# New instruction prices for the list scheduler of a one-layer hybrid encoder kernel

## The chip, the cores and the metric

The kernel runs on one core of one Trainium2 chip. The metric is the device time of one execution in microseconds; the figure given is the median over runs. A core has five engines that work from queues of their own, each in order: TensorE (matrix products), VectorE, ScalarE and GpSimd (elementwise work), and SyncE, which here issues the DMAs. In the profile they are PE (with PEld for the loading of weights), DVE, ACT, POOL and SP.

## The reference

One layer on 512 frames of width 1024, in float32. After an RMSNorm, one projection feeds three branches and their gates; the branches are merged, projected, added to the input, and a channel mixer follows:

```python
h = rmsnorm(x, norm_mix_g);  z = h @ w_in
# A: forgetting attention, 6 heads x 64, causal, bias from the summed log forget gates
logits = (q @ k.T) * scale + (c[:, None] - c[None, :]);  p = softmax(where(mask, logits, -inf))
# B: HGRN2, 4 heads, state 128 x 96, in chunks
attn = einsum(qx, kx, exp(b_t - b_s));  o = attn @ vx + (qx * exp(bx)) @ state
# C: gated input, causal depthwise convolution of width 31, LayerNorm, swish
merged = sigmoid(g0) * (ya @ wb0) + sigmoid(g1) * (yb @ wb1) + sigmoid(g2) * (yc @ wb2)
x = x + merged @ w_out
h2 = rmsnorm(x, norm_ffn_g);  gate, value = split(h2 @ w_up)
x = x + (silu(causal_dwconv3(gate)) * value) @ w_down
```

## The kernel before

Activations stand with channels on the 128 partitions and the 512 frames along the free dimension. Every large product is made in three float32r matmuls: weights and activations are split into a high and a low part, and high x high, high x low and low x high are summed in PSUM. A unit of weights (128 x 1024 float32) is loaded by a DMA (`wr_`), its high part is copied on ScalarE (`wh_`), and its low part is the difference on VectorE (`wl_`); one such unit feeds 24 matmuls of 512 columns, which fill one PSUM bank. VectorE then moves the bank to SBUF (`evac`) times the norm's factor.

The program has these stages. First the inputs are loaded and split, and the value product of the HGRN heads (`him`) runs with the norm's statistics. Then come the gated input of the convolution (`cb`, `ca`), the HGRN heads (`hf`, `hq`), the products of the attention (`f0`, `f1`, `fv`) and the output gate (`hg`). Beside these products the branches work on small tiles. An HGRN head (`hgrn_head`) takes exponentials and logarithms on ScalarE, a scan on VectorE (`b`), and then, for each of seven levels (the last without `d`), a difference on GpSimd (`d`), two exponentials on ScalarE (`ed`), two products on VectorE (`kl`, `ql`) and narrow float32 matmuls (`pl`). It also has a matmul on the products of first frames (`pr`, `pa`), transposes of `kh` (`khT`), and at the end `pi`. An attention head (`fox_head`) has differences on GpSimd (`dd`), `sp`, `ptp` and `po`. The convolution (`conv`) is 60 multiply-adds on VectorE (`cv`, the taps), started by two plain products. Then 24 gate products (`gl`), at most 18 of them ahead of the merges, the branch projections (`br`), the output projection (`wo`), the mixer (`ug`, `uv`) and the down projection (`dn`).

The order of all this is not written by hand. Class `Plan` records each instruction with its operands; `record` asks `cost` for two numbers, the time for which the instruction holds its engine and the time until others see its result. `schedule` then plays a list schedule: an instruction may start when its operands are there by these numbers, its engine is free, and the tiles that it is the first to write have a place under `CAPS`; among those that can start on an engine the lowest `pri` goes first. `pri` is the place in the program, less a large number for first loads (`FIRST`), weight preparation (`WPREP`), statistics and evacuation (`EVAC`). An instruction that can start is never held back for a more urgent one. `issue` emits the instructions in that order, and each engine and the DMA queue then run theirs in exactly that order, whatever the real durations are. All instructions are emitted from one line, so the profile shows nearly everything as L109 and is read by tile names.

Of the kernel before, what the change touches and what calls it, by code (L numbers as in the profile page):

```python
# [11 lines left out]
F32R = mybir.dt.float32r  # L12
# [51 lines left out]
class Plan:  # L64
    """Records the instructions, then issues them in the order of a list schedule.

    An instruction starts when its operands are there, its engine is free and the tiles that it
    is the first to write have a place; among those that can start, the lowest `pri` goes first.
    """

# [164 lines left out]
def cost(eng, name, outs, ins, args, kw):  # L235
    """Microseconds for which an instruction holds its engine, and until others see its result."""
    if name == "table":
        return 1.3, 0.1
    o = outs[0]
    n = 1  # L240
    for _, c in o.ap[1:]:
        n *= c
    hop = Plan.HOP
    if name == "dma_start":
        return max(0.45, o.ap[0][1] * n * 4 / 360e3), 2.1
    if eng == "tensor":
        wide = max(n, int(np.prod([c for _, c in ins[0].ap[1:]])))
        if name == "transpose":
            return 0.003 + wide * 0.835e-3, 0.3
        return 0.003 + wide * (0.4167e-3 if ins[0].dtype == F32R else 1.667e-3), 0.3  # L250
    psum = any(a.space == bass.MemoryType.PSUM for a in ins + outs)
    if eng == "scalar":
        aps = sum(isinstance(kw.get(k), bass.AP) for k in ("bias", "scale"))
        return (0.05 if psum else 0.1) + n * 0.833e-3 + 0.09 * aps + 0.087 * (kw.get("accum_out") is not None), hop
    if eng == "vector":
        aps = 0.058 * sum(all(c == 1 for _, c in a.ap[1:]) for a in ins) if n > 1 else 0.0
        if name in ("tensor_scalar", "tensor_copy", "memset", "tensor_single_scalar") and not psum:
            return 0.07 + n * 0.52e-3 + aps, hop
        if name == "reciprocal":
            return 0.07 + n * 6.2e-3, hop  # L260
        i = max([n] + [int(np.prod([c for _, c in a.ap[1:]])) for a in ins])
        return 0.07 + i * 1.04e-3 + aps, hop
    if name == "memset":
        return 0.06 + n * 0.8e-3, hop
    if name == "tensor_copy":
        return 0.1 + n * 3.5e-3, hop
    if any(s == 0 for a in ins for s, _ in a.ap[1:]):
        return 0.15 + n * 1.67e-3, hop
    return 0.15 + n * 2.1e-3, hop
# [3 lines left out]
def body(ctx: ExitStack, tc, xT, wct, wt3, wt1, wdn, par, cst, rst, msk, out):  # L273
# [9 lines left out]
    def nm(name):  # L283
        cnt[0] += 1
        return f"{name}_{cnt[0]}"
# [21 lines left out]
    def cc(name):  # L307
        o, w = CCOLS[name]
        return cs[:, o:o + w]

    ident, ones, big = cc("ident"), cc("ones"), cc("big")

# [1 line left out]
    def wunit(src, n, name, base=WPREP):  # L314
# [75 lines left out]
    def spread(cols, parts, name):  # L390
        """Columns [frame, (column of cols, block of frames)], each as a row that a run of partitions shares."""
        n = len(parts) * NM
        pt = bank(name + "rT")
        nc.tensor.transpose(pt[:n, :P], cols, ident)
        row = slot(name + "row")[:, :P]
        nc.vector.tensor_copy(row[:n], pt[:n, :P])
        dr = drp.tile([len(parts), NM, P], F32, name=nm(name + "dr"))
        nc.sync.dma_start(dr.rearrange("h m p -> (h m) p"), row[:n])
        t = slot(name + "rB")
        for u, (p0, p1) in enumerate(parts):  # L400
            nc.sync.dma_start(t[p0:p1], dr[u].rearrange("m p -> (m p)").unsqueeze(0).broadcast_to([p1 - p0, S]))
        return t
# [11 lines left out]

# [1 line left out]
    warm = slot("warm")  # L416
# [55 lines left out]

# [1 line left out]
    uus, first_sig = [], []  # L474
# [13 lines left out]

# [1 line left out]
    lbl = pc("lbl", 0, 4)  # L490
# [8 lines left out]
    lb = const("lbv", 4)  # L499
# [14 lines left out]

# [1 line left out]
    obs = []  # L516
# [6 lines left out]
    def hgrn_head(h, xf, xq):  # L523
# [4 lines left out]
        nc.vector.scalar_tensor_tensor(u, xf, 0.0, u, op0=ALU.min, op1=ALU.subtract)  # L528
        # forget gate: log f = logaddexp(log lb, log(1 - lb) + logsig)
        y = slot("y")  # L530
# [4 lines left out]
        nc.vector.tensor_tensor(lf, y, lf, op=ALU.add)  # L535
        # k = 1 - f
        kk = u
# [7 lines left out]
        nc.vector.tensor_tensor(qe, xq, eb, op=ALU.mult)  # L545
        # carried state
        kh = slot("kh")
# [16 lines left out]
        for c in range(1, NM - 1):  # L564
            nc.vector.scalar_tensor_tensor(st[:, c * HV:(c + 1) * HV], st[:, (c - 1) * HV:c * HV],
                                           eb[:, c * P + P - 1:c * P + P], pst[:, c * HV:(c + 1) * HV],
                                           op0=ALU.mult, op1=ALU.add)
        # attention inside a chunk, one level per power of two: in blocks of 2L frames the queries of
        # the second half see the keys of the first, and the first of those queries its own key
        at = ats[h % 2]  # L570
        atc = at.rearrange("p (c t) -> p c t", t=P)
        for li, L in enumerate(LEVELS):
# [20 lines left out]
            if L >= 32:  # L593
                # blocks that start at whole quadrants are taken one by one, and need no mask
                nb = P // (2 * L)
                for i in range(NM * nb):
                    nc.tensor.matmul(pl[:L + 1, i * L:(i + 1) * L], kl[:, 2 * i * L:2 * i * L + L + 1],
                                     ql[:, i * L:(i + 1) * L], start=True, stop=True)
                for i in range(nb):
                    o = 2 * i * L  # L600
                    nc.scalar.copy(atc[o:o + L + 1, :, o + L:o + 2 * L],
                                   pl[:L + 1, :S // 2].rearrange("p (c n l) -> p c n l", c=NM, l=L)[:, :, i])
                continue
            for c in range(NM):
# [6 lines left out]
                pl[:, :S // 2].rearrange("p (c n l) -> p c n l", c=NM, l=L))  # L611
        # the first frame of a chunk and its own key
        pr0 = tiny("pr0", NM)
# [41 lines left out]

# [1 line left out]
    tiles = ([], [])  # L657

    def fox_qk(qk):
# [23 lines left out]
        for j in range(3):  # L683
            pt = bank("qkT")
            for m in range(NM):
                nc.tensor.transpose(pt[:, m * P:(m + 1) * P], raw[m][:, j * P:(j + 1) * P], ident)
            # high parts of both heads, and for each head a tile with the high part in one half
            # of the partitions and the low part in the other
            one = slot(f"qk1{qk}{j}", F32R)
            two = [slot(f"qk2{qk}{j}", F32R) for _ in range(2)]  # L690
            if qk == 0:
                nc.scalar.activation(one, pt, AF.Copy, scale=g)
            for r, t in zip((0, FD), two):
                rs, ro = slice(r, r + FD), slice(FD - r, P - r)
                if qk == 0:
                    hi, lo = one[rs], t[rs]
                else:
                    hi, lo = t[rs], one[rs]
                    nc.scalar.activation(hi, pt[rs], AF.Copy, scale=g[rs])
                nc.vector.scalar_tensor_tensor(lo, pt[rs], g[rs], hi.bitcast(F32), op0=ALU.mult, op1=ALU.subtract)  # L700
                nc.vector.tensor_copy(t[ro], one[rs])
            tiles[qk].append((one, two))
# [5 lines left out]
    def fox_v():  # L708
        pss = gemm_t([wt1[u] for u in range(4)], FW + FH, "fv")
        lfx = tiny("lfx", NM * FH)  # L710
        for m, ps in enumerate(pss):
            with nc.at(EVAC):
                # even heads, then odd ones: high and low parts side by side, for the odd heads low parts first
                two = [slot(f"fv{m}{a}", F32R) for a in range(2)]
# [32 lines left out]
    def fox_head(h):  # L747
# [8 lines left out]
        last = []  # L756
        # the transposed weights of two blocks of queries lie side by side for each block of keys
        for i0 in (0, 2):
            ptps = [bank(f"ptp{h}{i0}{a}") for a in range(i0 // 2 + 1)]
            for i in (i0, i0 + 1):  # L760
# [12 lines left out]
                                               accum_out=mn)  # L773
# [15 lines left out]
            for k in range(i0 + 2):  # L789
                n = 2 * P if k <= i0 else P  # L790
                w = fv[k][h % 2][:, j * P:(j + 1) * P]
                for u in range(2):
                    with nc.after(*last):
                        op = nc.tensor.matmul(po[:, (i0 + 2) * P - n:(i0 + 2) * P], w,
                                              pts[k // 2][u][:, k % 2 * 2 * P:k % 2 * 2 * P + n],
                                              start=k == u == 0, stop=k == i0 + 1 and u == 1)
# [7 lines left out]

# [1 line left out]
    zs = []  # L806
# [45 lines left out]

# [1 line left out]
    hgrn_head(0, *hgrn_gemm(0))  # L854
# [32 lines left out]

# [1 line left out]
    bounds = ((0, 3), (3, 6), (6, 8))  # L889
# [33 lines left out]

# [1 line left out]
    acc2 = None  # L925
# [13 lines left out]

# [1 line left out]
    gT = []  # L941
# [14 lines left out]
    for n in range(KT):  # L956
        parts = ((0, S),) if n < KT - 1 else ((0, S // 2), (S // 2, S))
# [91 lines left out]
```

## Time and profile before

| | us |
|---|---|
| median of three runs | 843.89 |
| lowest, highest run | 841.92, 846.9 |
| profiled execution, first to last instruction | 844.6 |
| TensorE busy (PE) | 821.4 |
| VectorE busy (DVE) | 512.6 |
| ScalarE busy (ACT) | 333.2 |
| GpSimd busy (POOL) | 161.5 |

The profile is of one execution, and gives no other time of it than this span. Busy time is the time in which an engine had an instruction in work; a busy TensorE is not one at its peak. The granted clock (PEclk) is the share of TensorE's full clock that it was given in a stretch.

### The profile page before, as it was taken

To read this page: it belongs to the slowest core of one execution; us is meant where nothing else is said; L and a number is where in the kernel's file an instruction comes from. 1 tells how busy PE (TensorE), PEld (TensorE's weight loads), DVE (VectorE), ACT (ScalarE), POOL (GpSimd) and SP (SyncE) were. 2 spreads that over 40 slices of the span, in tenths; PEclk is the share of its full clock that TensorE was granted. 3 is DMA by queue.
4 is the path that set the end of the run, shared out by engine and by line. 5 is a ranking of instruction groups with operands and counts; after the bars stand their busy time and mean duration, and the time that the engine had idled before them with its cause. 6 is when DMAs were issued, how large, how long until landed. Compare 5 with 4: busy or idle time off the path is not lost.

```text
span 844.6 us, 10337 instructions
## 1 busy us (share of the span) xinstructions
PE 821.4 (97%) x3979; PEld 690.2 (82%) x3979; DVE 512.6 (61%) x813; ACT 333.2 (39%) x536; POOL 161.5 (19%) x144
## 2 busy tenths in 40 slices
PE   6998989999999999999999999999999999999998
PEld 5887989867777788888888888888888888888888
DVE  6589998998877873355664456555555555322221
ACT  6235464645555653333233334333333333212110
POOL 4215040055542200011352311111100111000000
PEclk9998999989999999999999999999999999999999
DMA  6622122321111232223443223233332223333320
GB/s 214 193 75 70 49 66 76 104 90 46 63 64 58 68 100 94 92 103 112 137 137 100 99 88 100 100 100 101 100 100 89 92 94 94 109 103 119 119 82 26
DMA packets 26238, 80.74 MB, mean 96 GB/s; under 512 B 2982, under 2 KB 3782, under 8 KB 26188
## 3 DMA queue, kind: packets, MB, share of 16 engines
q1 hardware_dynamic: 26188, 80.08, 29.2%
q8 instruction: 31, 0.51, 0.3%
q14 instruction: 19, 0.16, 0.1%
HBM read 77.94 MB, written 2.13 MB: 95 GB/s over the span
## 4 chain that ended last, share of the span: by engine, by line
PE 87%; DVE 9%; issue 2%; ACT 1%; DMA 1%; POOL 0%; SPq 0%; DVEq 0%
PE gl L109 15%; PE dn L109 14%; PE ug L109 14%; PE uv L109 14%; PE wo L109 5%; PE br L109 5%; PE pl L109 2%; PE fvm L109 2%; PE hg L109 2%; PE sp L109 2%; DVE qk L109 1%; PE cb L109 1%; PE ca L109 1%; PE hf L109 1%; DVE cv L109 1%
## 5 line engine op out<-in xcount | busy, mean ns | idle before, releaser
L109 POOL TENSOR_TENSOR fy<-fy,n2rB 128x512 f32<-128x512 f32 x22 | 29.2, 1328 | 207.4 <-ACT fy L109 207.4
L109 DVE TENSOR_TENSOR wl_wd<-wr_wd,wh_wd 128x1024 fp32r<-128x1024 f32 (+1 forms) x24 | 27.3, 1136 | 65.8 <-ACT wh_wd L109 65.8
L109 DVE TENSOR_TENSOR wl_ug<-wr_ug,wh_ug 128x1024 fp32r<-128x1024 f32 x22 | 27.2, 1237 | 53.5 <-ACT wh_ug L109 53.5
L109 ACT CAST wh_wd<-wr_wd 128x1024 fp32r<-128x1024 f32 (+1 forms) x24 | 23.5, 980 | 85.7 <-PE dn L109 81.9
L109 ACT CAST wh_gl<-wr_gl 128x1024 fp32r<-128x1024 f32 x24 | 25.2, 1050 | 59.8 <-issue 49.7
L109 POOL TENSOR_TENSOR gr<-gr,gr 128x512 f32<-128x512 f32 x16 | 25.1, 1567 | 123.5 <-DVE gr L109 122.7
L109 DVE TENSOR_TENSOR gr<-gl,n1rB 128x512 f32<-128x512 f32 x24 | 16.6, 691 | 50.4 <-PE gl L109 50.2
L109 DVE SCALAR_TENSOR_TENSOR cv<-xca,pr,cv 128x511 f32<-128x511 f32 (+29 forms) x60 | 46.5, 780 | 0.2
L109 ACT CAST wh_uv<-wr_uv 128x1024 fp32r<-128x1024 f32 x22 | 23.2, 1053 | 45.6 <-PE ug L109 38.2
L109 POOL TENSOR_TENSOR d<-b 128x512 f32<-128x512 f32 x24 | 34.3, 1453 | 17.8 <-DVE b L109 9.3
L109 ACT CAST wh_ug<-wr_ug 128x1024 fp32r<-128x1024 f32 x22 | 23.1, 1050 | 27.6 <-PE uv L109 21.2
L109 DVE TENSOR_TENSOR wl_gl<-wr_gl,wh_gl 128x1024 fp32r<-128x1024 f32 x24 | 31.5, 1311 | 3.2 <-ACT wh_gl L109 2.7
L109 POOL TENSOR_TENSOR dd<-cB,cq 128x128 f32<-128x128 f32 (+3 forms) x24 | 18.7, 783 | 76.1 <-DMA cB<-cdr 50.4
L109 DVE SCALAR_TENSOR_TENSOR fy<-ug,pr,fy 128x511 f32<-128x511 f32 (+1 forms) x44 | 32.6, 747 | 0.7
L109 DVE TENSOR_TENSOR ug<-ug,n2rB 128x512 f32<-128x512 f32 x22 | 15.2, 692 | 28.9 <-PE ug L109 27.3
L109 ACT ACTIVATE fy<-fy 128x512 f32<-128x512 f32 x22 | 13.9, 632 | 41.3 <-DVE fy L109 41.3
L109 DVE TENSOR_TENSOR wl_uv<-wr_uv,wh_uv 128x1024 fp32r<-128x1024 f32 x22 | 27.0, 1225 | 4.2 <-ACT wh_uv L109 4.2
L109 PEld LDWEIGHTS pl<-ql,kl 128*128 128x128 f32 (+2 forms) x224 | 21.9, 171 | 5.6 <-POOL d L109 3.9
L109 PE MATMUL pl<-ql,kl 128*128 128x64 f32 (+2 forms) x224 | 22.6, 254 | 3.3 <-DVE ql L109 3.2
L109 DVE TENSOR_TENSOR x<-dn,x 128x512 f32<-128x512 f32 (+1 forms) x9 | 5.7, 632 | 27.8 <-PE dn L109 27.8
L109 DVE TENSOR_TENSOR gr<-gr,br 128x512 f32<-128x512 f32 x24 | 16.2, 683 | 6.7 <-PE br L109 6.7
L109 DVE TENSOR_TENSOR kl<-ed,u 128x260 f32<-128x260 f32 (+6 forms) x28 | 17.4, 621 | 3.3 <-issue 3.0
(1128 smaller groups left out, 2654.4 us busy)
## 6 DMA issues: line engine op xcount, KB each, us to landing
wr_gl<-wct SPq DMA_DIRECT2D x24, 512.0 KB, 3.3
wr_ug<-wct SPq DMA_DIRECT2D x22, 512.0 KB, 3.3
wr_uv<-wct SPq DMA_DIRECT2D x22, 512.0 KB, 3.2
wr_wd<-wdn SPq DMA_DIRECT2D x16, 512.0 KB, 3.5
x<-xT SPq DMA_DIRECT2D x16, 256.0 KB, 3.6
wr_wb<-wct SPq DMA_DIRECT2D x8, 512.0 KB, 3.4
wr_wo<-wct SPq DMA_DIRECT2D x8, 512.0 KB, 3.3
wr_wd<-wdn SPq DMA_DIRECT2D x8, 384.0 KB, 3.1
```

What stands on the lines that cost most here:

```text
L109: op.fn = lambda: fn(*args, **kw)
```

## The change

It changes the numbers that `cost` gives for VectorE, ScalarE and the wide matmuls, and gives the scan a price of its own. The other lines of the diff take out comments. Prices of GpSimd and of the DMAs, the delay until others see a result, the priorities and the caps stay.

```diff
...
-        return 0.003 + wide * (0.4167e-3 if ins[0].dtype == F32R else 1.667e-3), 0.3
+        if ins[0].dtype == F32R:
+            return 0.013 + wide * 0.4167e-3, 0.3
+        return 0.003 + wide * 1.667e-3, 0.3
     psum = any(a.space == bass.MemoryType.PSUM for a in ins + outs)
     if eng == "scalar":
         aps = sum(isinstance(kw.get(k), bass.AP) for k in ("bias", "scale"))
-        return (0.05 if psum else 0.1) + n * 0.833e-3 + 0.09 * aps + 0.087 * (kw.get("accum_out") is not None), hop
+        return (0.143 if psum else 0.187) + n * 0.833e-3 + 0.09 * aps + 0.087 * (kw.get("accum_out") is not None), hop
     if eng == "vector":
         aps = 0.058 * sum(all(c == 1 for _, c in a.ap[1:]) for a in ins) if n > 1 else 0.0
         if name in ("tensor_scalar", "tensor_copy", "memset", "tensor_single_scalar") and not psum:
-            return 0.07 + n * 0.52e-3 + aps, hop
+            return 0.155 + n * 0.52e-3 + aps, hop
         if name == "reciprocal":
-            return 0.07 + n * 6.2e-3, hop
+            return 0.145 + n * 6.2e-3, hop
+        if name == "tensor_tensor_scan":
+            return 0.145 + n * 2.08e-3, hop
         i = max([n] + [int(np.prod([c for _, c in a.ap[1:]])) for a in ins])
-        return 0.07 + i * 1.04e-3 + aps, hop
+        return 0.155 + i * 1.04e-3 + aps, hop
...
```

## Rows read from the trace of the kernel before

**Rows 1.** The head of the page.

```profile
span 844.6 us, 10337 instructions
```

**Rows 2.** Windows by stage: stretch, length, busy (count) PE, PEld, DVE, ACT, POOL; PEclk, DMA, GB/s.

```profile
0.00:20.00 20.00, 13.96 (x62) 11.75 (x62) 13.01 (x15) 14.59 (x23) 7.88 (x10) 1.00 0.68 226
20.00:306.00 286.00, 272.04 (x1491) 233.00 (x1492) 247.92 (x499) 146.15 (x305) 86.73 (x90) 0.95 0.25 79
306.00:840.00 534.00, 534.00 (x2417) 444.26 (x2417) 251.20 (x300) 172.44 (x210) 66.86 (x45) 1.00 0.31 100
840.00:844.60 4.60, 1.43 (x12) 1.22 (x11) 0.42 (x1) 0.00 (x0) 0.00 (x0) 0.99 0.08 29
```

**Rows 3.** Windows of 20 us between 20 and 306 us, the same columns.

```profile
20.00:40.00 20.00, 19.32 (x92) 17.56 (x93) 11.40 (x19) 5.21 (x8) 7.17 (x9) 0.91 0.59 188
...
60.00:80.00 20.00, 16.14 (x93) 14.38 (x92) 19.74 (x25) 11.26 (x22) 10.96 (x7) 0.91 0.23 73
80.00:100.00 20.00, 20.00 (x129) 19.00 (x128) 18.98 (x39) 9.91 (x23) 0.00 (x0) 0.92 0.21 61
...
120.00:140.00 20.00, 17.78 (x123) 16.71 (x123) 17.54 (x37) 11.13 (x26) 3.18 (x3) 0.91 0.23 73
...
160.00:180.00 20.00, 18.34 (x90) 14.71 (x87) 19.61 (x29) 12.23 (x18) 6.23 (x7) 1.00 0.29 95
180.00:200.00 20.00, 19.57 (x90) 14.52 (x91) 16.66 (x31) 10.86 (x26) 11.49 (x9) 0.74 0.20 64
200.00:220.00 20.00, 17.15 (x98) 13.54 (x97) 20.00 (x36) 10.30 (x32) 15.14 (x17) 1.00 0.16 55
220.00:240.00 20.00, 19.91 (x148) 18.02 (x148) 15.43 (x38) 9.79 (x26) 7.39 (x12) 0.92 0.13 42
...
280.00:300.00 20.00, 18.25 (x89) 14.81 (x88) 18.64 (x43) 14.49 (x24) 4.70 (x3) 1.00 0.29 93
```

**Rows 4.** Waits of TensorE over the span: us in total, times, longest.

```profile
PE pl L109 <- DVE ql L109: 3.2, 2, 2.3
...
PE pa L109 <- DVE pr L109: 2.8, 2, 2.1
...
PE khT L109 <- DVE kh L109: 2.2, 1, 2.2
```

**Rows 5.** Timeline of TensorE in 174 to 190 us: start, us, instruction [idle before].

```profile
180.43 0.19 PE L109 MATMUL pa<-pr,cs 128*1 128x4 f32 x2 [2.09 <-DVE pr L109]
180.55 0.50 PE L109 MATMUL hq<-x6l,wh_hq 128*128 128x512 f32 x1
```

**Rows 6.** Groups by form: out<-in, shapes, count | busy us, mean ns | idle before.

```profile
L109 DVE TENSOR_TENSOR wl_uv<-wr_uv,wh_uv 128x1024 fp32r<-128x1024 f32 x22 | 27.0, 1225 | 4.2 <-ACT wh_uv L109 4.2
...
L109 DVE TENSOR_TENSOR gr<-gl,n1rB 128x512 f32<-128x512 f32 x24 | 16.6, 691 | 50.4 <-PE gl L109 50.2
...
L109 DVE TENSOR_TENSOR ql<-ed,xq 128x256 f32<-128x256 f32 x24 | 13.8, 574 | 0.0
...
L109 DVE TENSOR_TENSOR_SCAN b<-reset,lf 128x512 f32<-128x512 f32 x4 | 4.9, 1213 | 0.0
...
L109 ACT CAST wh_gl<-wr_gl 128x1024 fp32r<-128x1024 f32 x24 | 25.2, 1050 | 59.8 <-issue 49.7 <-PE gl L109 6.4 <-PE hg L109 3.7
...
L109 POOL TENSOR_TENSOR d<-b 128x512 f32<-128x512 f32 x24 | 34.3, 1453 | 17.8 <-DVE b L109 9.3 <-PE sp L109 4.3 <-DVE rl L109 2.7
```

**Rows 7.** The chain that ended last: start, us, what.

```profile
305.98 54.41 PE gl L109 x240
360.40 5.44 PE br L109 x24
```

**Rows 8.** Timelines of VectorE and GpSimd in 46 to 82 us.

```profile
74.20 0.94 DVE L109 TENSOR_TENSOR kl<-ed,u 128x260 f32<-128x260 f32 x1 [0.26 <-ACT ed L109]
75.06 1.29 DVE L109 TENSOR_TENSOR ql<-ed,xq 128x256 f32<-128x256 f32 x1
...
70.01 9.66 POOL L109 TENSOR_TENSOR d<-b 128x512 f32<-128x512 f32 x6 [4.00 <-DVE b L109]
```

## The prediction

> **What bounds the kernel now.** I read the span first [rows 1]: 844.6 us for the profiled execution. The page gives no other time of that execution, so the sum is made against this span. The three timed runs have a median of 843.89, 0.7 less than the span and well inside their own 5 us of spread, so I carry a difference from the one to the other unchanged.
>
> Then the windows by stage [rows 2]. The reader is to see that the span has two parts that behave differently. From 306 to 840 us TensorE is busy for 534.00 of 534.00 us at a granted clock of 1.00, while VectorE is busy for 251.20 and ScalarE for 172.44. Nothing there waits, so no order of VectorE or ScalarE work can shorten it; only something that makes TensorE wait can lengthen it. From 20 to 306 us TensorE is busy for 272.04 of 286.00 us, and VectorE for 247.92. So 13.96 us of TensorE idle time lie here, and the clock averages 0.95. The first 20 us have 6.04 us more of idle time, with the DMA share at 0.68: that is loading.
>
> Next the same part in stretches of 20 us [rows 3]. Two prices stand in each row: idle time (20 less PE busy) and lost clock (20 times one less PEclk). Paired by place, a clock loss going with the stall before it:
> - head, 20 to 40: 0.68 + 1.8 = 2.5
> - A, 60 to 100: 3.86 + 1.8 + 1.6 = 7.3
> - B, 120 to 140: 2.22 + 1.8 = 4.0
> - C, 160 to 200: 1.66 + 0.43 + 5.2 = 7.3
> - D, 200 to 240: 2.85 + 0.09 + 1.6 = 4.5
> - E, 280 to 300: 1.75 and no clock loss
>
> The sum is 27.4 (some 0.4 of idle time lies in stretches not shown). A granted clock below 1.00 in these averages is time at the lower of two levels, 1.2 instead of 2.4 GHz, and in these rows it shows in a stretch in which TensorE had stood or in the next one. So a stalled microsecond costs about two: 13.96 idle and 13.8 lost clock.
>
> Last, what the stalls wait for [rows 4]: small results of VectorE, the ql, pr and kh of the HGRN heads. The timeline of C shows how it happens [rows 5]: two tiny matmuls on pr hold TensorE for 2.09 us, and behind them stands hq, whose operands are there. TensorE takes its queue in order; the planner had put pa ahead of hq because, by its prices, pr was ready by then.
>
> **The change part by part.** No operation, priority, tile or dependence changes. Only the prices by which the list schedule orders the queues do. I check each against a row [rows 6].
>
> VectorE's fixed part rises by 0.085 (0.075 for reciprocal and scan). A 128x512 product: old 0.07 + 512 x 1.04e-3 = 0.602, new 0.687, row 691 ns. A 128x1024 low part: new 1.220, row 1225. The scan: old 0.602, new 0.145 + 512 x 2.08e-3 = 1.210, row 1213. ScalarE: a 128x1024 cast was 0.953, now 1.040, row 1050. The wide matmul: old 0.003 + 512 x 0.4167e-3 = 0.2163, new 0.2263; 24 of them take 5.44 us [rows 7], 0.2267 each. So the new prices are those of instructions that run undisturbed.
>
> What the old prices hid in the middle part: 499 VectorE instructions x 0.085 = 42.4 us, on an engine that really works 247.92 of 286 us, against at most 1491 x 0.010 = 14.9 us of TensorE. VectorE fell behind TensorE by the difference, less its own idle time (38.1 us), and wherever it was behind, a branch matmul put "just in time" became a stall. The planner also filled gaps of VectorE that did not exist with taps of the convolution (60 of them, non-preemptive), ahead of work that TensorE was to wait for. With true prices those taps go later, the branch matmuls move back in TensorE's queue, and GEMM work fills in front of them. The filler is there: after 306 us ten units of gl run alone for 54.41 us before the first br [rows 7]; any of them can be taken earlier at no cost.
>
> What the change leaves wrong: GpSimd's prices, and any instruction that is stretched by a neighbour. A d of 128x512 has a broadcast operand and is priced 0.15 + 512 x 1.67e-3 = 1.005; its row says 1453 ns, 0.448 more, 24 times: 10.8 us. A ql of 128x256 is now priced 0.421 and takes 574 on the mean, 0.153 more, 24 times: 3.7 us. The timeline of A shows the bad case [rows 8]: while GpSimd runs six d in a row for 9.66 us, a kl of 260 columns takes 0.94 us (price 0.425) and a ql 1.29 (price 0.421), two and three times their prices.
>
> The Trainium skill (GPSIMD Engine Reference, 1. Specifications) says that GpSimd shares its SBUF interfaces with VectorE and that they contend when the VectorE instruction reads two SBUF inputs. The trace agrees with that as far as [rows 8] go. By that rule, no fixed price per instruction can place the kl and ql of a head rightly, and the stalls at the bursts would stay; its time is worked out as the second rival.
>
> So by stretch. B, C and E go: GpSimd is busy there for 3.18, 6.23 and 11.49, and 4.70 of 20 us, mostly less than in A and D (10.96 and 15.14), and the lag is mainly the one that the new prices know: -(4.0 + 7.3 + 1.75) = -13.05. Bounds: 0 if every one moves elsewhere, -13.05 if all go. A and D: the unpriced part remains. I take half of 7.3 + 4.5, so -5.9; bounds 0 and -11.8, half because these stretches hold both causes. Head: loading sets it; 0, bounds -2.5 and +2.5. New stalls that the new order makes: the trace cannot show them. Bounds 0 and 29.0 (10.8 + 3.7 unpriced, doubled for the clock); I take 6, near the price of one stall like A or C, since the order must change in hundreds of places and the four bursts stay. From 306 us on: 0, hidden under 534 us of matmuls; if the cover failed, one late low part would cost up to its own 1.225 us per unit. Prices of ScalarE: 0 by themselves, because ScalarE is busy for only 146.15 of 286 us; without that cover the cost would be a just-in-time stall as above, in the same terms.
>
> Sum: -13.05 - 5.9 + 6 = -13, so 831 us.
>
> **Rivals.**
>
> First, everything goes: all of A to E (24.9), no new stall: 844.6 - 24.9 = 820. For it: the filler of 54.41 us, and that no wait of TensorE but those on small VectorE results is long in this part. Against it: the 14.5 us unpriced.
>
> Second, the stalls only move. The unpriced 10.8 + 3.7 = 14.5 us reach TensorE whole, doubled by the clock: 29.0 against the 27.4 of today, so 846, no change. For it: [rows 8] is where A lies, and a list schedule leaves a branch matmul no slack. Against it: VectorE has 38.1 us of idle time in which lag can be absorbed, and GpSimd is busy for only 86.73 of these 286 us [rows 2].
>
> Third, slower: the taps of the convolution move out of the HGRN heads, VectorE then does kl and ql close together, right under the bursts of d, and every one of the four heads pays what A pays now: 4 x 7.3 = 29.2. With the head (2.5) and one long clock loss like the 5.2 of C this is 36.9 against 27.4, so 854 us. It decides from 24.9 / 4 = 6.2 us per head on; below that the kernel is not slower. For it: A is the costliest stall of today together with C, and is of this kind. Against it: D is also under a burst, the longest one, and costs 4.5. A second way to slower is weaker: VectorE priced full, the branches end so late that gl is used up. The branches would have to end 54.41 us later, more than the 42.4 that all new VectorE prices add; it has 0.02 within the chance below.
>
> **How the numbers follow.** A measurement of this kernel can tell about 0.5% from no change, here 4.2 us, so faster means below 839.7 and slower above 848.1. The forecast (gain of 5 to 20 us) has 0.48, the first rival 0.14, both faster: 0.62. The second rival has 0.20, the third 0.18. The range: the first rival's 820 lies near the low end; 818 leaves about 0.05 below, for a shorter head. Above, half of the third rival's 0.18 lies over 850. So 818 to 850, with the forecast's own range 825 to 839.
>
> **What would show it.** Right: in the part before the long run of gl, idle time of TensorE falls from 13.96 to about 8, the clock of that part rises above 0.95, and fewer stretches show it below 1.00; the waits on pr and kh vanish, those on ql shrink but stay; the taps of the convolution lie later; the run of pure gl before the first br is shorter than 54.41 us because some of it was used as filler; from there to the end nothing changes. Wrong in step: stalls of the B and C kind persist although VectorE's prices now fit (then VectorE's fixed part was not their cause), or kl and ql are stretched in all four heads (third rival), or TensorE is seen idle after the branches. The whole is wrong if the idle time and the clock loss fall and the span does not: then TensorE's busy time has grown by as much, through more changes between narrow and wide matmuls, which I price at nothing.

## The result, and the profile after

The kernel with the new prices takes 831.18 us (median of 4 runs, 830.0 to 832.68) against 845.33 (841.92 to 846.9) beside it: a ratio of 0.9844 with a 95% interval of 0.9809 to 0.9879. It is faster by 1.6%, and the forecast was 831. The profiled execution has a span of 830.0 us, so 14.6 of it are to be explained.

The windows of 20 us of the kernel after, with the columns of [rows 3]: stretch, length, busy time and count of PE, PEld, DVE, ACT, POOL, then PEclk, DMA share, GB/s.

```profile
0.00:20.00 20.00, 15.54 (x75) 14.10 (x76) 11.76 (x17) 13.85 (x21) 4.51 (x7) 1.00 0.72 240
20.00:40.00 20.00, 17.68 (x90) 15.20 (x89) 10.60 (x17) 6.49 (x11) 12.46 (x12) 1.00 0.53 177
...
60.00:80.00 20.00, 16.75 (x97) 15.58 (x95) 19.97 (x24) 9.91 (x18) 10.75 (x7) 0.99 0.25 85
80.00:100.00 20.00, 20.00 (x134) 18.32 (x134) 16.79 (x37) 11.05 (x27) 0.00 (x0) 0.93 0.19 57
...
120.00:140.00 20.00, 20.00 (x149) 19.62 (x148) 17.82 (x36) 11.19 (x28) 2.59 (x3) 1.00 0.30 106
...
160.00:180.00 20.00, 19.37 (x80) 14.59 (x79) 19.55 (x27) 9.75 (x14) 6.91 (x7) 0.91 0.24 82
180.00:200.00 20.00, 18.73 (x110) 14.68 (x109) 17.40 (x28) 11.84 (x28) 13.56 (x11) 1.00 0.20 67
200.00:220.00 20.00, 18.26 (x127) 15.18 (x127) 20.00 (x39) 11.47 (x33) 10.29 (x10) 1.00 0.16 53
220.00:240.00 20.00, 20.00 (x127) 16.66 (x126) 19.48 (x41) 10.12 (x29) 12.60 (x19) 1.00 0.17 54
...
280.00:300.00 20.00, 19.66 (x103) 15.74 (x102) 17.44 (x34) 14.00 (x27) 5.15 (x3) 1.00 0.20 70
```

The stretch of 120 to 140 us has no stall left (17.78 us busy before, [rows 3]), and PEclk is below 1.00 only in or right behind the stalls at 60 to 80 and at 160 to 180 us. VectorE is as busy as before, 512.4 us in all against 512.6: its work is the same, only its order differs. Over the first 460 us TensorE is idle for 14.0 us (20.0 before), and the mean granted clock of the span is 0.996 (0.984), so lost clock is 830.0 x 0.004 = 3.3 us against 13.5. The clock gave back more (10.2 us) than the idle time did (6.0 us).

What TensorE waited for in the kernel after (us in total, times, longest):

```profile
PE him L109 <- ACT wh_hi L109: 3.3, 2, 2.3
PE pl L109 <- DVE ql L109: 2.5, 3, 1.4
PE n1ms L109 <- POOL n1sq L109: 2.3, 1, 2.3
PE khT L109 <- DVE kh L109: 1.9, 1, 1.9
...
PE pa L109 <- DVE mn L109: 0.6, 1, 0.6
```

The wait on pr [rows 4] is gone, and those on ql are shorter. The wait on kh of [rows 4] lay at 120 to 140 us and is gone too, but another kh now makes TensorE wait for 1.9 us at 60 to 80 us. In the head the wait for the norm's statistics on GpSimd is new, in place of one on wl_hi.

The chain of the kernel after, around the first br:

```profile
296.25 16.18 PE gl L109 x71
312.43 0.44 PE cvt L109 x4
312.87 13.86 PE gl L109 x61
...
328.54 17.24 PE gl L109 x76
345.78 5.44 PE br L109 x24
```

The first br starts at 345.78 us instead of 360.40 [rows 7]: 14.6 us earlier, which is the whole gain. From there to the end both kernels take 484.2 us. The gates are now broken up by work of the convolution (cvt, ycT), because its taps run later. The tile cv in the kernel before, then in the kernel after (duration ns least/median/most, first and last start):

```profile
L109 DVE SCALAR_TENSOR_TENSOR cv<-xca,pr,cv x60: 697/733/1517, 45.7 to 215.5; 128x511 f32<-128x511 f32 x2, 128x510 f32<-128x510 f32 x2, 128x509 f32<-128x509 f32 x2, 128x508 f32<-128x508 f32 x2
```

```profile
L109 DVE SCALAR_TENSOR_TENSOR cv<-xca,pr,cv x60: 706/732/1779, 47.6 to 310.2; 128x511 f32<-128x511 f32 x2, 128x510 f32<-128x510 f32 x2, 128x509 f32<-128x509 f32 x2, 128x508 f32<-128x508 f32 x2
```

The last tap starts at 310.2 instead of 215.5 us.

### The profile page after: what moved, and what is told of

It is laid out like the page before. It is cut to its first block, busy times and chain, and to the rows that moved or that the text cites. A ratio compares the mean times of both kernels' runs of the same rounds, so it can differ in the third digit from the quotient of the medians.

```text
span 830.0 us, 10340 instructions
## 1 busy us (share of the span) xinstructions
PE 812.9 (98%) x3979; PEld 683.0 (82%) x3979; DVE 512.4 (62%) x813; ACT 332.7 (40%) x536; POOL 168.4 (20%) x144
## 4 chain that ended last, share of the span: by engine, by line
PE 89%; DVE 6%; issue 2%; POOL 1%; DMA 1%; ACT 1%; SPq 0%; DVEq 0%; POOLq 0%
PE gl L109 15%; PE dn L109 15%; PE ug L109 14%; PE uv L109 14%; PE wo L109 5%; PE br L109 5%; PE fvm L109 2%; PE pl L109 2%; PE f1m L109 2%; PE hf L109 2%; PE hq L109 2%; PE sp L109 2%; PE f0m L109 1%; PE ca L109 1%; PE cb L109 1%
## 5 line engine op out<-in xcount | busy, mean ns | idle before, releaser
L109 DVE SCALAR_TENSOR_TENSOR cv<-xca,pr,cv 128x511 f32<-128x511 f32 (+29 forms) x60 | 49.0, 827 | 0.2
L109 POOL TENSOR_TENSOR dd<-cB,cq 128x128 f32<-128x128 f32 (+3 forms) x24 | 22.0, 923 | 66.9 <-DVE u L109 38.2
L109 ACT ACTIVATE ed<-d 128x256 f32<-128x256 f32 x48 | 18.5, 413 | 5.5 <-POOL d L109 2.0
```

The costliest lines, as they stand in the source:

```text
L109: op.fn = lambda: fn(*args, **kw)
```

## The experiments

Theory L: instructions of VectorE took longer than planned, so results came later than their place in TensorE's queue, and each such lateness became a stall and a loss of clock. Rivals: the matmul price (P), ScalarE's price (S), the nearness of each price to the trace as such (A), an unlucky order before, against which any new one gains (C), and others named where they apply. Each kernel was timed in five rounds against the kernel before.

**One part alone.** The kernel before with one of the three groups of new prices.

```diff
-            return 0.07 + n * 0.52e-3 + aps, hop
+            return 0.155 + n * 0.52e-3 + aps, hop
...
-        return 0.07 + i * 1.04e-3 + aps, hop
+        return 0.155 + i * 1.04e-3 + aps, hop
```

> Only VectorE's prices are the new ones. Theory L (VectorE's lag against its plan is what became stalls): nearly the whole gain is here; ratio 0.978 to 0.988 to the kernel before, idle time of TensorE up to the first br about 14 us against 20.0, at most two stretches at 1.2 GHz. Rival P (the matmul price paces the plan): ratio 0.995 to 1.005. Rival S (ScalarE): the same, 0.995 to 1.005. Rival C (any new order would do, the order before was an unlucky one): 0.98 to 1.00, not telling by itself.

```diff
-        return (0.05 if psum else 0.1) + n * 0.833e-3 + 0.09 * aps + 0.087 * (kw.get("accum_out") is not None), hop
+        return (0.143 if psum else 0.187) + n * 0.833e-3 + 0.09 * aps + 0.087 * (kw.get("accum_out") is not None), hop
```

> Only ScalarE's prices are the new ones. Theory L: ScalarE has idle time in the first part, its price alone moves little; ratio 0.993 to 1.003. Rival S: 0.98 to 0.988. Rival C: anywhere in 0.98 to 1.00, as likely as in the other single edits.

```diff
-        return 0.003 + wide * (0.4167e-3 if ins[0].dtype == F32R else 1.667e-3), 0.3
+        if ins[0].dtype == F32R:
+            return 0.013 + wide * 0.4167e-3, 0.3
+        return 0.003 + wide * 1.667e-3, 0.3
```

> Only the wide matmul's price is the new one. Theory L: TensorE then no longer runs behind its plan, so VectorE's lag of 42 us stands against it without the 15 us of cover; no gain, ratio 0.998 to 1.01. Rival P: 0.98 to 0.99. Rival C: 0.98 to 1.00.

VectorE's prices (with reciprocal and scan, as in the change) give 0.9798 (0.9768 to 0.9828), the matmul's 0.9989 (0.9973 to 1.0005): as L has it, and P falls. ScalarE's give 0.9907 (0.9883 to 0.9931), more than L expected; that expectation was wrong. It is less than S asked for, and VectorE's prices have the whole gain without them, so S falls as the main cause. In the trace with ScalarE's prices alone TensorE is idle for 13.0 us from 20 to 460 us, nearly as before (14.0); what is better is the first 20 us (2.7 us idle instead of 6.0) and the lost clock (8.3 instead of 13.5). The middle part of the kernel with VectorE's prices, and its last 160 us up to 460:

```profile
20.00:300.00 280.00, 274.36 (x1545) 234.04 (x1546) 234.75 (x462) 148.56 (x308) 87.94 (x91) 1.00 0.26 85
300.00:460.00 160.00, 160.00 (x713) 132.38 (x712) 99.81 (x138) 55.18 (x70) 36.62 (x22) 1.00 0.33 111
```

5.6 us of idle time are left there, and no loss of clock. Up to 460 us it is idle for 10.0 us, less than the 14 expected.

**Is any other order better?** Another small change to the plan, in both directions.

```diff
-    HOP = 0.27
+    HOP = 0.30
```

> The kernel before with all its prices, but the time until others see a result is 0.30 instead of 0.27: a small change of another kind, which makes another order. Theory L: lag of VectorE unchanged, ratio 0.993 to 1.007. Rival C (any new order gains): 0.98 to 0.99.

> The kernel before with 0.24 instead of 0.27 until others see a result, the mirror of x4_before_hop30 (0.30 gave 0.994). Theory L: results are promised earlier still, VectorE's chain is later against its plan: not faster, 0.998 to 1.012. Rival C (the order before was an unlucky one, any new order gains): faster again, 0.98 to 0.995.

With 0.30 the ratio is 0.9943 (0.9924 to 0.9963), with 0.24 it is 0.997 (0.995 to 0.9989). Both gain a little; the longer delay stays within L's bounds, the shorter one falls just outside them. So the order before was a slightly unlucky one, worth some 0.3 to 0.6%; that is far from 1.6 or 2%, and C does not carry the result.

**The change without the matmul's price.** VectorE's and ScalarE's edits above, TensorE's line as before.

> VectorE's and ScalarE's new prices, the wide matmul at its old one: the change less one part. x1_dve_only (0.980) beat the whole change (0.984), x2_act_only had 0.991. Theory L: a TensorE priced 15 us too fast in the first part makes the plan late for TensorE, which covers VectorE's unpriced lag; so this is at least as fast as the whole change, 0.975 to 0.984. Rival A (prices nearer to the trace are better, each of them): slower than the whole change, 0.985 to 0.99.

0.9787 (0.9762 to 0.9812): level with VectorE's prices alone, so ScalarE's add nothing on top of them. Its median is 826.88 us against the change's 831.18; the intervals of the two ratios touch (0.9809 to 0.9812), so that the true matmul price costs half a per cent is likely and not certain. Two stretches in which the change stalls are nearly free of stalls here:

```profile
60.00:80.00 20.00, 19.80 (x109) 18.41 (x108) 18.99 (x25) 11.07 (x20) 8.56 (x6) 1.00 0.29 93
160.00:220.00 60.00, 59.96 (x349) 49.15 (x347) 54.71 (x97) 35.57 (x79) 33.12 (x29) 1.00 0.24 78
```

Rival A, that every price nearer to the trace helps, falls for the matmul's. I tested L's reason for it, lost cover, with a margin on the whole change:

```diff
-    HOP = 0.27
+    HOP = 0.30
```

> The whole change, and 0.30 instead of 0.27 until others see a result. The whole change stands at 0.984, the change without the matmul price (x5_no_pe_price) at 0.979. Theory L: a true matmul price takes away the cover for VectorE's unpriced lag; a margin of 0.03 on each result, which gave 0.994 on the kernel before, gives cover back: 0.977 to 0.982, with less idle time at 60 to 80 and 160 to 220 us than the 6.9 us of the change. Rival O (the difference is the luck of one order): anywhere in 0.98 to 0.99.

It came out at 0.9872 (0.9851 to 0.9892), outside the 0.977 to 0.982 that L gave it, and slower than the change, if anything. Its windows:

```profile
20.00:40.00 20.00, 15.51 (x67) 12.88 (x66) 10.28 (x17) 5.79 (x9) 11.84 (x12) 0.85 0.52 169
60.00:80.00 20.00, 20.00 (x108) 18.49 (x106) 19.96 (x29) 11.46 (x21) 6.62 (x4) 1.00 0.28 92
160.00:220.00 60.00, 57.66 (x298) 45.53 (x297) 54.99 (x93) 34.82 (x73) 31.66 (x29) 1.00 0.26 85
```

The two stalls that were named did shrink (60 to 80 us: 3.25 to 0; 160 to 220 us: 3.64 to 2.34). But 20 to 40 us now has 4.5 us idle and a clock of 0.85, on two waits of the norm's statistics, and 100 to 160 us has 2.4 us of new idle time:

```profile
PE n1ms L109 <- POOL n1sq L109: 2.3, 1, 2.3
PE n1rT L109 <- DVE nry L109: 2.2, 1, 2.2
```

So the stalls fell where the margin was aimed, and the new order lost more elsewhere; lost cover is not shown, and the luck of one order (O) is not excluded. What the runs do show together: the two kernels with the new matmul price beside VectorE's lie at 0.984 and 0.987, while six with VectorE's prices at 0.155 to 0.20 and the old matmul price lie at 0.979 to 0.980, whatever else was varied. Why stays open.

**GpSimd's prices**, which the change leaves as they were, on top of VectorE's.

```diff
-        return 0.15 + n * 1.67e-3, hop
-    return 0.15 + n * 2.1e-3, hop
+        return 0.35 + n * 1.67e-3 + 0.22 * (len(o.ap) > 2), hop
+    return 0.25 + n * 2.5e-3, hop
```

> x1_dve_only with GpSimd's prices also set to the rows (a broadcast product 0.35 + n x 1.67e-3, 0.22 more for d; others 0.25 + n x 2.5e-3), which the change left low by 10.8 us for d. Theory L: the stalls at the HGRN bursts were unpriced lag, so idle time of TensorE between 60 and 220 us falls below that of x1_dve_only (some 4 us) and the ratio is 0.972 to 0.980. Rival D (what remains is VectorE stretched beside GpSimd, which no price of GpSimd knows): as x1_dve_only, 0.978 to 0.983.

0.9798 (0.9772 to 0.9823), the same as without, and idle time at 60 to 220 us did not fall (5.3 us, 4.3 without). So L's forecast of fewer stalls there failed, and the 10.8 us by which the prediction called d priced too low were not what the rest of the stalls came from, at least not by themselves. The ratio lies in the ranges of both L and rival D; the idle time speaks for D. The lengths of d in the kernel before suggest why a higher price is no better one:

```profile
L109 POOL TENSOR_TENSOR d<-b x24: 1035/1275/3396, 70.0 to 215.3; 128x512 f32<-128x512 f32 x24
```

The shortest takes 1.035 us, close to the old price of 1.005. The mean of 1.453 is pulled up by longer ones, so no fixed price fits all 24.

**Price beyond the trace.** VectorE's fixed part at 0.24 and at 0.18, and at 0.20 with the convolution recorded earlier:

```diff
-            return 0.155 + n * 0.52e-3 + aps, hop
+            return 0.24 + n * 0.52e-3 + aps, hop
...
-        return 0.155 + i * 1.04e-3 + aps, hop
+        return 0.24 + i * 1.04e-3 + aps, hop
```

> x1_dve_only with VectorE's fixed part at 0.24 (0.23 for reciprocal and scan), as far above the trace as the old price was below it. Theory L with margin: VectorE is never later than its plan, so stalls fall further or stay; 0.972 to 0.983. Rival A (a price near the trace is best): clearly worse than x1_dve_only, above 0.986, with the branches planned so late that gl runs out or the conv ends after the gates.

> x1_dve_only with VectorE's fixed part at 0.18 (0.17) instead of 0.155 (0.145): between the trace's price and x8_dve_over's 0.24, which ended the stalls before 300 us but pushed the last tap of the convolution to 380 us. Theory L: the stalls shrink and the last tap ends before the gates are used up: 0.973 to 0.981. Rival A: above 0.982.

```diff
     for h in range(FH):
+        if h == 4:
+            conv()
         fox_head(h)
-    conv()
```

> VectorE's fixed part at 0.20 (0.19), and the convolution recorded before the last two attention heads, so that its taps have the better priority there. If x8_dve_over lost by the late convolution alone, this keeps its freedom from stalls before 300 us without the idle 11.6 us at 360 to 400: 0.970 to 0.981. If a plan that fills VectorE too much starves TensorE whatever waits last: above 0.985, with idle time moved to the attention's last heads.

At 0.24 the whole gain is gone: 0.999 (0.997 to 1.001), as A has it. The windows tell why:

```profile
360.00:400.00 40.00, 28.38 (x108) 20.51 (x107) 30.02 (x55) 7.54 (x10) 2.98 (x2) 0.86 0.18 61
...
20.00:300.00 280.00, 277.56 (x1534) 237.35 (x1532) 215.97 (x412) 129.74 (x266) 82.85 (x84) 1.00 0.28 90
```

Up to 300 us this is the best order of all, 2.4 us idle and no loss of clock. Then TensorE stands for 11.6 us between 360 and 400. Its chain there:

```profile
375.56 0.72 DVE cv L109
...
388.88 0.69 DVE gr L109
389.57 0.09 DVE cra L109
...
392.54 0.55 DVE ctok L109
393.10 0.04 issue
393.14 1.85 PE ycT L109 x7
...
397.25 0.63 ACT ycT0h L109
```

The taps, the filler of VectorE's queue, went so late (last start 379.6 us) that the gates were used up before the LayerNorm of the convolution was done: 7.0 of the 11.6 us are the waits on ctok and ycT0h. The rest waits for weights to be prepared, part of it behind a tap. Both ends have their own loss: priced too low, the branches stall; priced too high, the convolution does. Between them it is flat: 0.18 gives 0.9799 (0.9773 to 0.9825), 0.20 with the earlier convolution 0.9796 (0.977 to 0.9821). With the latter TensorE is idle for only 0.6 us between 300 and 460 us, as the first reading of that run's expectation has it. But the freedom from stalls before 300 us, which that reading wanted kept, was not: 6.3 us are idle from 20 to 300 us, and 6.6 with 0.18, against 2.4 at 0.24 and 5.6 at 0.155. So the ratios came as expected and the stalls did not shrink. 0.20 without the earlier convolution was not run.

**A margin on the delay instead**, VectorE at 0.155:

```diff
-    HOP = 0.27
+    HOP = 0.60
```

> x1_dve_only (0.980) with 0.60 instead of 0.27 until others see a result: a margin on the delay of every result that does not fill VectorE's time. Theory L (a stall is a result later than planned): the stalls on small VectorE results up to the first br shrink below x1_dve_only's (some 5 us without the first 20 us), ratio 0.973 to 0.980, and the conv stays off the path since VectorE is not priced fuller. Rival A (any price off the trace costs): above 0.984.

0.9802 (0.9774 to 0.9829), no better than without, and waits on kh grew to 2.9 us (0.4 without) where I expected less. L's forecast of fewer stalls failed (7.0 us idle from 20 to 300 us, 5.6 without), and so did A's of a loss. The margin neither helps nor hurts.

**The ledger.** For each profiled execution: idle time of TensorE in the first 460 us, lost clock (span times one less the mean granted clock), and what is left of the span. All in us.

| kernel | ratio | span | idle | lost clock | rest |
|---|---|---|---|---|---|
| before | 1 | 844.6 | 20.0 | 13.5 | 811.1 |
| the change | 0.9844 | 830.0 | 14.0 | 3.3 | 812.7 |
| x1 VectorE alone | 0.9798 | 824.4 | 10.0 | 1.6 | 812.8 |
| x2 ScalarE alone | 0.9907 | 834.5 | 15.7 | 8.3 | 810.5 |
| x3 matmul alone | 0.9989 | 840.8 | 19.9 | 6.7 | 814.2 |
| x4 delay 0.30 | 0.9943 | 837.3 | 18.5 | 6.7 | 812.1 |
| x5 without matmul | 0.9787 | 826.9 | 10.2 | 5.0 | 811.7 |
| x6 delay 0.24 | 0.997 | 842.2 | 16.0 | 11.8 | 814.4 |
| x7 with GpSimd | 0.9798 | 827.1 | 12.7 | 1.7 | 812.7 |
| x8 VectorE 0.24 | 0.999 | 841.2 | 18.9 | 6.7 | 815.6 |
| x9 delay 0.60 | 0.9802 | 828.1 | 12.6 | 3.3 | 812.2 |
| x10 VectorE 0.18 | 0.9799 | 827.0 | 12.4 | 1.7 | 812.9 |
| x11 0.20, conv | 0.9796 | 827.6 | 12.3 | 1.7 | 813.6 |
| x12 change, 0.30 | 0.9872 | 833.7 | 14.9 | 5.8 | 813.0 |

The rest varies by 5 us, idle time and lost clock together by 22: fourteen orders of the same instructions differ almost only in how long TensorE stands and how long it runs slow after that.

## Why the prediction was right

The mechanism held: VectorE's prices alone carry the gain, it shows as stalls and lost clock ahead of the first br, and nothing after it moved. The second rival (the stalls only move) and the third (all heads pay what A paid) did not come, though a piece of each is in the trace. The wait on kh turns up in A, and the mean of a ql rose (that the taps no longer keep kl and ql out of the bursts of GpSimd is my reading of it, not tested). From the groups of the kernel after, the answer to the ql of [rows 6]:

```profile
L109 DVE TENSOR_TENSOR ql<-ed,xq 128x256 f32<-128x256 f32 x24 | 15.7, 652 | 0.0
```

That is 652 ns against 574, for 24 of them 1.9 us.

Of the terms of the sum, some were wrong and cancelled. From the windows after, priced in the same way:
- B, C and E were to go whole, -13.05. B went (-4.0). C fell from 7.3 to 0.63 + 1.27 + 1.8 = 3.7 (-3.6), E from 1.75 to 0.34 (-1.4). Together -9.0: C was mis-sized, since stalls of small VectorE results remain there. The reason for putting it with B, little GpSimd work, does not hold by the prediction's own rows: GpSimd is busy for 11.49 us in C's second half, more than the 10.96 of A. Like A and D together, C fell by about half. What makes its stalls was not isolated.
- A and D were to fall by half, -5.9. A fell from 7.3 to 3.25 + 0.2 + 1.4 = 4.9, D from 4.5 to 1.74: -5.2. In A the idle time itself fell little (3.86 to 3.25): the waits on ql and pr went from 3.9 to 1.4, and the new one on kh took 1.9 us back.
- The head was to stay. Its first 20 us lost 1.6 us of idle time and its next 20 us went from 2.5 to 2.3: -1.8. The stall there is another one (n1ms for wl_hi).
- New stalls were to cost 6. Outside the head no stretch stalls that did not stall before; the new waits, 1.9 us on kh in A and three of 0.6 or 0.7 us in C and D, are in the sums above. The rest of the ledger, for which the sum has no other term, grew by 1.6.

The sum is -9.0 - 5.2 - 1.8 + 1.6 = -14.4, and 0.4 of idle time at 100 to 120 us went too. So 831 was hit in part by luck: 4 us too many at B, C and E met an allowance 4.4 us too large.

Four things the prediction reasoned wrongly. It thought ScalarE's prices worth nothing by themselves; alone they gave 0.991, and what they do in the plan was not traced. It doubled each stalled microsecond; from 20 to 306 us idle time fell by 4.4 (13.96 to 9.56, where about 8 was forecast) and lost clock over the span by 10.2. Its sum for VectorE's lag shows none: 42.4 less 14.9 is 27.5, and less 38.1 of VectorE's idle time that is below zero. The lag is a local one, in stretches like those of A, C and D in which VectorE is busy for 19.6 to 20.0 of 20 us [rows 3]. And it blamed what would be left in part on a low price of d; a higher one changed nothing, and the old price is close to the shortest d.

What does stretch an instruction shows in VectorE's timeline of the kernel after, at the burst of d in A (70.07 to 79.10 us):

```profile
72.07 2.08 DVE L109 TENSOR_TENSOR wl_hf<-wr_hf,wh_hf 128x1024 fp32r<-128x1024 f32 x1
...
76.94 1.27 DVE L109 TENSOR_TENSOR kl<-ed,u 128x260 f32<-128x260 f32 x1
78.13 1.25 DVE L109 TENSOR_TENSOR ql<-ed,xq 128x256 f32<-128x256 f32 x1
79.30 0.42 DVE L109 TENSOR_TENSOR kl<-ed,u 128x264 f32<-128x264 f32 x1
79.65 0.41 DVE L109 TENSOR_TENSOR ql<-ed,xq 128x256 f32<-128x256 f32 x1
79.98 1.22 DVE L109 TENSOR_TENSOR wl_hq<-wr_hq,wh_hq 128x1024 fp32r<-128x1024 f32 x1
```

During the burst a low part takes 2.08 us and behind it 1.22, a kl 1.27 and 0.42, a ql 1.25 and 0.41: 0.84 to 0.86 us more each, whatever its own length. A ql thus takes three times as long, a low part not twice. It does not hit every instruction: in the next burst (114.16 to 122.59 us) a low part of 780 columns takes 0.97 us, as right behind that burst. The Trainium skill (GPSIMD Engine Reference, 1. Specifications) says that VectorE and GpSimd share SBUF interfaces and contend for them when a VectorE instruction has two SBUF inputs. The trace agrees with that as far as these lengths go. But the stalls did not all stay, as the second rival would have had it: beside the burst at 114.16 us TensorE does not stall at all; it is busy for all of 100 to 140 us.

The weaker way to slower, gl used up before the branches end, was given 0.02; with prices that fit, it did not come, but x8 shows that it is real: 11.6 us idle and a ratio of 0.999. The cover shrank with the change too, from 54.41 us of gl alone ahead of the first br to 17.24.

## What to carry to other kernels

Where a planner fixes the order of queues that run in order, compare its price of each kind of instruction with the trace, first on the engine that is nearly full beside the bound one: a constant 0.085 us too little on VectorE cost 2%. Nearer to the trace is not better for every engine: the true matmul price added nothing here and may have cost half a per cent. Do not add margin by pricing that engine fuller than it is, since filler work then moves so late that it becomes the path; from 0.155 to 0.20 the time was flat (0.20 with the convolution recorded earlier), at 0.24 the gain was gone. Take the mean of a kind apart before it becomes a price: here d and ql ran from a shortest length to three times that. Count the clock that a stall may cost beside the stall itself, and expect different orders of equal merit to lie up to half a per cent apart.

## What the runs showed of the hardware

Lost clock does not follow idle time in proportion. Before, 20.0 us idle went with 13.5 us of lost clock; with VectorE's prices alone 10.0 us idle went with 1.6; the kernel with matmul prices alone had the idle time of before (19.9) and half of its lost clock (6.7). So the amount of idle time alone does not set the lost clock: over the fourteen kernels it was between an eighth and three quarters of the idle time. What else sets it was not isolated.

A VectorE product of two SBUF tensors beside a burst of GpSimd's d took some 0.85 us more than right behind it, at 256 columns (1.25 against 0.41 us) as at 1024 (2.08 against 1.22 us). In another burst one of 780 columns took no longer than behind it (0.97 us both).
